# A decoder layer in split fp32: order at the end of the up projection, order of operand sums and accumulating transfers in the down pass

## The chip, the cores and the metric

The kernel runs on one core of a Trainium2 chip. The metric is the device time of one execution in microseconds (us). A core has five engines that run side by side, each through a queue of its own in order: TensorE (PE in the profile) multiplies matrices, VectorE (DVE) and ScalarE (ACT) work on rows, GpSimd (POOL) does elementwise work and issues transfers, and SyncE (SP) issues most transfers. An instruction that waits on a semaphore holds all that stands behind it on its engine. In the profile a group of instructions is named by line, engine, operation and `out<-in`.

## The reference

One step of a hybrid decoder layer: 1024 prompt rows and 64 sample rows, width 1024, feed-forward width 2816, all in fp32. Attention comes first; what matters here is the feed-forward part and the layer's end:

```python
def conv_ffn(n, prev, lw):
    a = n @ lw['ffn_w_gate']
    c = n @ lw['ffn_w_up']
    T = a.shape[1]
    full = jnp.concatenate([prev.astype(a.dtype), a], axis=1)
    w = lw['ffn_conv_w']
    conv = lw['ffn_conv_b'] + sum(w[j] * full[:, j:j + T] for j in range(CONV_W))
    y = (jax.nn.silu(conv) * c) @ lw['ffn_w_down']
    return y, full[:, full.shape[1] - (CONV_W - 1):]
...
    y, conv_new = conv_ffn(rmsnorm(h, lw['g_ffn']), conv_prev, lw)
    h = h + y
    h = h + (p.astype(h.dtype) @ lw['ple_w_proj']) * jax.nn.sigmoid(rmsnorm(h, lw['g_ple']) @ lw['ple_w_gate'])
```

The first product is called the gate branch (it passes the convolution and the silu), the second the up branch. The prompt and the sample rows go through the same layer.

## The kernel before

**Arithmetic.** PE multiplies in a reduced form of fp32, so each fp32 operand is split in two: ACT casts it to a rounded high part, and DVE (now and then POOL) subtracts that from the source to leave the residue, the low part (`split`, L114; the DVE line is L116). `mm3` (L137) then makes one product of three matmuls: high with high (L138), high with low (L139), low with high (L140).

**Up projection.** `ff_chunk(f)` (L1753) handles 128 of the 2816 columns at a time, 22 chunks. The prompt rows go by a Strassen-like scheme of products `m1` to `m7` of 384 columns each, into PSUM tiles `ps_gu`; the rows that the scheme leaves over (256 of the prompt and 64 of the sample, 320 columns) go through `rest`, once for the gate branch and once, as `pu`, for the up branch. `conv` and silu give `cv`; it is multiplied by the up branch and written to DRAM as `ds[f]`. The 64 sample columns are split into `ssm`, and a chunk later PE multiplies them by the split weights `wdh`, `wdl` into `ps_ds` (`sample_weights`, `sample_rows`, L1751). After the last chunk its own sample rows follow at the very end of the up projection: PE's last work there is `m3`, `m7`, `m4`, then the 24 matmuls of `pu`, then four `ps_ds` matmuls, which need `ssm`.

**Down pass.** y is computed by a Strassen-like scheme too: seven products, in the order of `SEVEN`: 1, 5, 6, 3, 7, 2, 4. Each runs over `NK` = 11 steps `k`, and a step is 12 matmuls of 512 columns into four PSUM tiles `ps_dn` (four row tiles, three matmuls each). I write p7 for product 7. A step has four parts:

- `load(p, k)`: SP issues two transfers of 256 KB (rows of `ds`, rows of `ffn_w_down`; three in p5). In p1 they go into one of eleven lasting tiles `st2`, for the other products into a ring of five tiles `raw2` (both read `st` and `raw` in the profile).
- `operands(p, k)`: in p5, p6, p3, p7 and p4 DVE first makes a sum or difference of the new tile and `st2` (L1942, L1943, L1948, L1952 among others), and then `split` makes the operand `o`: a cast of 128x1024 on ACT, a residue of 128x1024 on DVE. `o` has four places.
- `summed`: the matmuls.
- `folded` and `folded_on`: after a product DVE (ACT for some) adds the PSUM tiles into `h`.

`residue(i, j, t)` (L1969) is a GpSimd-issued transfer that adds 256 KB from DRAM (`dhp`, the residual stream) to a tile of `h` that was folded. There are 16 of them, and a tuple of four entries (product, first step, i, j) says where they stand in the program: four each, on every second step, in p6, p3, p7 and p2. `fold_sample` brings the sample rows' `ps_ds` into `hs` (a COPY `fd` on ACT, two additions `hs` on DVE); it stands at p1, step 1.

**Order.** The kernel is built with a scheduler that simulates a time line: it keeps the dependencies, gives each engine's instructions an order of its own and sets the waits. `tc.issue_after(x)` adds a dependency for order alone. Loads are issued four steps ahead in the program and operands two steps ahead, but on each engine the scheduler decides what really stands ahead of what.

```python
        if i + 4 < len(steps):
            load(*steps[i + 4])
        if i + 2 < len(steps):
            operands(*steps[i + 2])
```

Of the kernel before, what the change touches and what calls it, by code (L numbers as in the profile page):

```python
# [44 lines left out]
def step_kernel(ctx: ExitStack, tc: tile.TileContext, A):  # L45
# [66 lines left out]
        return r  # L112

    def split(hi, lo, src, lo_eng=None):  # L114
        act.copy(hi, src)  # L115
        (lo_eng or dve).tensor_tensor(lo, src, hi.bitcast(F32), ALU.subtract)  # L116

    def norm_rows(wk, x, rows, gb, out=None):
        junk = wk.tile([P, D], BF16, tag="sqd", name="junk", bufs=1)
# [246 lines left out]
    def sample_weights():  # L366

        hl = [cp.tile([P, 8, P], F32R, tag="craw", name="wqe", bufs=3).rearrange("p a c -> p (a c)")[:, 0:768]
              .rearrange("p (k c) -> p k c", k=2) for _ in range(3)]
        l1 = [cp.tile([P, 512], F32R, tag="csq", name="wql", bufs=2)[:, 0:384] for _ in range(2)]  # L370
        wq = []
        for f in range(2):
            hi = [hl[2 * f][:, k] for k in range(2)]
            lo = [l1[k] if f else hl[1][:, k] for k in range(2)]
            for k in range(2):
                raw = wp.tile([P, 384], F32, tag="stage", name="stage", bufs=3)
                sp.dma_start(raw, A["mla_w_qup"][0][k * P:(k + 1) * P, f * 384:(f + 1) * 384])
                split(hi[k], lo[k], raw, pool)
            wq.append((hi, lo))
        return wq  # L380
# [1372 lines left out]
    def ff_chunk(f):  # L1753
        tp = z["tp"]
        w = wgu.pop(f)
        a = tp.tile([P, 2 + T + 80], F32, tag=f"a{f % 2}", name="a", bufs=1)
        a_s = a[:, 2 + T:].rearrange("p (b t) -> p b t", t=10)
        cv = tp.tile([P, NTOK], F32, tag=f"cv{f % 2}", name="cv", bufs=1)
        cvs = cv[:, T:].rearrange("p (b t) -> p b t", t=8)
        w3 = [convT[:, j * NF + f:j * NF + f + 1] for j in range(4)]  # L1760

        def conv(n0, n1):
            dve.tensor_scalar(cv[:, n0:n1], a[:, n0:n1], w3[0], w3[3], ALU.mult, ALU.add)
            for j in (1, 2):
                dve.scalar_tensor_tensor(cv[:, n0:n1], a[:, n0 + j:n1 + j], w3[j], cv[:, n0:n1], ALU.mult, ALU.add)
# [34 lines left out]
        dve.tensor_tensor(a[:, 2 + NP:2 + 2 * NP], m3, q, ALU.add)  # L1800
        m7 = product("s3", "t3")
        dve.tensor_tensor(v, m7, v, ALU.add)
        pool.tensor_tensor(m5c, m5c, v, ALU.add)
        if late:
            sample_rows(late.pop(0), 1)
        sample_weights(f, 1)
        m4 = product("u1", "t4")
        dve.tensor_tensor(v, m4, v, ALU.add)
# [4 lines left out]
        pool.tensor_tensor(cv[:, 0:NP], cv[:, 0:NP], v, ALU.mult)  # L1813
        conv(NP, T)
        dve.tensor_scalar(cvs, a_s[:, :, 0:8], w3[0], w3[3], ALU.mult, ALU.add)
        for j in (1, 2):
            dve.scalar_tensor_tensor(cvs, a_s[:, :, j:j + 8], w3[j], cvs, ALU.mult, ALU.add)
        pool.tensor_copy(cout[:, 0:2, f], a[:, T:T + 2])
        pool.tensor_copy(cout[:, 2:18, f].rearrange("p (b j) -> p b j", j=2), a_s[:, :, 8:10])
        act.activation(cv[:, NP:], cv[:, NP:], AF.Silu)  # L1820
        pool.tensor_tensor(cv[:, NP:2 * NP], cv[:, NP:2 * NP], m5c, ALU.mult)
        dve.tensor_tensor(cv[:, 2 * NP:], cv[:, 2 * NP:], pu[:, :NR], ALU.mult)
        (pool if f == NF - 1 else sp).dma_start(ds[f], cv[:, 0:T])
        ss_ = tp.tile([P, P], F32R, tag="ssm", name="ssm", bufs=2)
        if f == NF - 1:
            dve.tensor_copy(ss_[:, 0:R], cv[:, T:])
        else:
            act.copy(ss_[:, 0:R], cv[:, T:])
        dve.tensor_tensor(ss_[:, R:2 * R], cv[:, T:], ss_[:, 0:R].bitcast(F32), ALU.subtract)
        chunks[f] = ss_  # L1830
        late.append(f)

# [81 lines left out]
    def cols_of(e, j, k):  # L1914
# [5 lines left out]
    st, src, opd, acc = {}, {}, {}, {}  # L1920

    def place_of(k):
        return f"st{(k + 3) % NK}"
# [14 lines left out]
    def operands(p, k):  # L1938

        (r, x), s2 = src.pop((p, k)), st[k]  # L1940
        if p == 5:
            dve.tensor_tensor(s2[:, 1], r[:, 1], s2[:, 1], ALU.subtract)  # L1942
            dve.tensor_tensor(s2[:, 0], r[:, 0], x, ALU.add)  # L1943
        elif p == 6:
            dve.tensor_tensor(s2[:, 1], r[:, 1], s2[:, 1], ALU.subtract)
            dve.tensor_tensor(s2[:, 0], s2[:, 0], r[:, 0], ALU.subtract)
        elif p == 7:
            dve.tensor_tensor(r, r, s2, ALU.subtract)  # L1948
        elif p == 4:
            dve.tensor_tensor(r[:, 1], r[:, 1], s2[:, 1], ALU.subtract)  # L1950
        elif p == 3:
            dve.tensor_tensor(r[:, 0], r[:, 0], s2[:, 0], ALU.subtract)  # L1952
        o = oroom()
        split(o[:, 0], o[:, 1], s2 if p in (5, 6) else r)
        opd[p, k] = o

    def banks(n):

# [1 line left out]
        return [b([P, 512], "ps_dn") for b in kinds]  # L1960

    def summed(p, k, t):
        o, tt = opd[p, k], slice(t * P, t * P + P)
# [93 lines left out]
    for i, (p, k) in enumerate(steps):  # L2057
# [169 lines left out]
```

## Time and profile before

| what | value |
| --- | --- |
| time, three runs | 2222.29, 2226.15, 2227.77 us, median 2226.15 |
| the profiled execution | 2226.47 us, its span 2224.8 us |
| mean granted TensorE clock | 0.983 |
| PE busy | 2136.6 us, 96% of the span |
| DVE, ACT, POOL busy | 1664.0, 1368.8, 1228.6 us |
| up projection ends, down pass ends, on PE | about 1872.7 us, about 2086 us |

The profile is one execution with a time stamp for each instruction. The span is the time from its first to its last record; the other 1.7 us of the execution lie around it. The view of windows gives, for each engine, its busy time and its number of instructions in a stretch, then the granted clock, the mean busy share of the 16 DMA engines and the GB/s that they moved. The time line lists instructions in order of start with the idle time ahead of them in brackets, and what ended it. SPq, DVEq and so on are an engine's sequencer.

### The profile page before, as it was taken

Reading aid. Unit: us, or ns where it says so; the run is one execution under the profiler, and the core shown is the slowest. Engines: PE = TensorE matmul, PEld = TensorE weight load, DVE = VectorE, ACT = ScalarE, POOL = GpSimd, SP = SyncE. Lnnn points to the kernel's source line nnn. Section 1 sums busy time; section 2 is a strip of 40 time slices with the busy share of each in tenths; the row PEclk is TensorE's granted clock in tenths of the full one; section 3 lists DMA queues with packets and bytes.
Section 4 is the critical chain, followed back from the end, with each engine's and each line's share of the span. In section 5 each row is a group of like instructions: output and inputs, shape, how many; then the busy total and the mean of one; then the engine's idle time right before and its main releaser. Section 6 shows DMA issues by size and latency. Waiting matters only on the chain.

```text
span 2224.8 us, 38405 instructions
## 1 busy us (share of the span) xinstructions
PE 2136.6 (96%) x13460; PEld 1932.1 (87%) x13460; DVE 1664.0 (75%) x2551; ACT 1368.8 (62%) x3726; POOL 1228.6 (55%) x1330
## 2 busy tenths in 40 slices
PE   7999989999999999999999987999999999999999
PEld 6889978878888888887888976999999998887899
DVE  4675666467788888886878778888888886976642
ACT  6576766777778888887767766333333333533631
POOL 5675668576777767777445547656565662010100
PEclk9899999999999999999999988999999999999999
DMA  5343235412342222221522212332232225958321
GB/s 181 109 142 108 77 120 157 138 54 76 96 119 72 65 60 60 61 58 52 169 69 72 70 67 91 100 104 87 96 94 93 93 91 178 298 163 233 109 70 41
DMA packets 204419, 233.07 MB, mean 105 GB/s; under 512 B 42423, under 2 KB 146340, under 8 KB 204228
## 3 DMA queue, kind: packets, MB, share of 16 engines
q1 hardware_dynamic: 188259, 179.49, 25.9%
q0 software_dynamic: 14736, 46.67, 7.4%
q10 hardware_dynamic: 1232, 4.46, 0.5%
q8 instruction: 108, 1.77, 0.3%
q14 instruction: 84, 0.68, 0.1%
HBM read 188.00 MB, written 42.52 MB: 104 GB/s over the span
## 4 chain that ended last, share of the span: by engine, by line
PE 77%; DVE 8%; ACT 5%; POOL 3%; DMA 3%; issue 2%; SPq 0%; ACTq 0%; DVEq 0%; POOLq 0%
PE ps_gu L139 7%; PE ps_gu L140 7%; PE ps_gu L138 7%; PE ks L138 5%; PE ks L140 4%; PE ks L139 4%; PE ps_dn L139 2%; PE ps_dn L140 2%; PE ps_dn L138 2%; PE cpv L644 2%; PE ctp L521 2%; PE ps_pj L138 2%; PE ps_lt L277 2%; PE ps_pj L139 2%; PE ps_pj L140 2%
## 5 line engine op out<-in xcount | busy, mean ns | idle before, releaser
L559 ACT ACTIVATE csq<-ks 128x256 f32<-128x256 f32 x1040 | 392.5, 400 | 87.1 <-PE ks L140 76.2
L564 DVE TENSOR_REDUCE css<-csq 128x16 f32<-128x1024 f32 (+1 forms) x264 | 315.7, 1196 | 64.3 <-ACT csq L559 61.4
L115 ACT CAST wh<-st 128x512 fp32r<-128x512 f32 x176 | 108.4, 619 | 187.5 <-PE ps_gu L139 167.8
L138 PE MATMUL ks<-mv1h,cTh 128*128 128x320 f32 (+1 forms) x520 | 170.0, 329 | 8.3 <-ACT sn L561 3.6
L138 PE MATMUL ks<-mv0h,cTh 128*128 128x320 f32 (+1 forms) x520 | 171.1, 331 | 7.0 <-ACT sn L561 3.0
L603 POOL TENSOR_TENSOR chl<-craw,chl 128x1024 fp32r<-128x1024 f32 x64 | 141.3, 2207 | 57.4 <-ACT chl L602 55.6
L139 PE MATMUL ks<-mv1l,cTh 128*128 128x320 f32 (+1 forms) x520 | 153.6, 297 | 0.0
L139 PE MATMUL ks<-mv0l,cTh 128*128 128x320 f32 (+1 forms) x520 | 152.4, 295 | 0.0
L140 PE MATMUL ks<-mv0h,cTl 128*128 128x320 f32 (+1 forms) x520 | 148.0, 297 | 0.9 <-DVE cTl L116 0.8
L140 PE MATMUL ks<-mv1h,cTl 128*128 128x320 f32 (+1 forms) x520 | 148.3, 299 | 0.0
L629 POOL TENSOR_TENSOR phl<-sn,phl 128x512 fp32r<-128x512 f32 (+1 forms) x64 | 85.0, 1328 | 105.5 <-ACT phl L628 104.9
L116 DVE TENSOR_TENSOR wl<-st,wh 128x512 fp32r<-128x512 f32 x132 | 119.0, 903 | 27.1 <-ACT wh L115 27.1
L116 POOL TENSOR_TENSOR wl<-st,wh 128x512 fp32r<-128x512 f32 x44 | 69.5, 1582 | 103.7 <-ACT wh L115 103.7
L139 PE MATMUL ps_dn<-o 128*128 128x512 f32 x308 | 120.6, 392 | 1.8 <-DVE o L116 1.8
L140 PE MATMUL ps_dn<-o 128*128 128x512 f32 x308 | 120.2, 390 | 0.0
L116 DVE TENSOR_TENSOR cTl<-ctp,cTh 128x512 fp32r<-128x512 f32 (+1 forms) x136 | 90.1, 662 | 38.9 <-ACT cTh L115 37.9
L138 PEld LDWEIGHTS ks<-mv1h,cTh 128*128 128x128 f32 x520 | 99.3, 191 | 20.8 <-ACT sn L561 7.7
L138 PEld LDWEIGHTS ks<-mv0h,cTh 128*128 128x128 f32 x520 | 98.2, 189 | 21.1 <-ACT sn L561 7.6
L561 ACT COPY sn<-ks 128x64 f32<-128x64 f32 x520 | 116.5, 224 | 0.0
L1316 POOL TENSOR_TENSOR pl<-p,ph 128x512 fp32r<-128x512 f32 (+1 forms) x96 | 97.5, 1020 | 30.2 <-DVE ph L1315 20.8
L138 PE MATMUL ps_dn<-o 128*128 128x512 f32 x308 | 111.1, 390 | 1.2 <-ACT o L115 1.2
L140 PE MATMUL ps_gu<-xrh,wl 128*128 128x320 f32 x352 | 108.7, 309 | 0.0
(672 smaller groups left out, 7873.3 us busy)
## 6 DMA issues: line engine op xcount, KB each, us to landing
raw<-ds SPq DMA_DIRECT2D x77, 256.0 KB
raw<-ffn_w_down SPq DMA_DIRECT2D x66, 256.0 KB
stage<-w_in SPq DMA_DIRECT2D x48, 256.0 KB
st<-ffn_w_gate SPq DMA_DIRECT2D x44, 256.0 KB
st<-ffn_w_up SPq DMA_DIRECT2D x44, 256.0 KB
wr<-ffn_w_down SPq DMA_DIRECT2D x44, 256.0 KB
ds<-cv SPq DMA_DIRECT2D x21, 512.0 KB
oraw<-doT SPq DMA_DIRECT2D x16, 256.0 KB
```

The costliest lines, as they stand in the source:

```text
L115: act.copy(hi, src)
L116: (lo_eng or dve).tensor_tensor(lo, src, hi.bitcast(F32), ALU.subtract)
L138: pe.matmul(ps, ah, bh, start=first, stop=False)
L139: pe.matmul(ps, ah, bl, start=False, stop=False)
L140: return pe.matmul(ps, al, bh, start=False, stop=last)
L277: pe.matmul(ps, x, w, start=first, stop=last)
L559: act.activation(sq[:, f * 256:f * 256 + 256], ks[:, 0:256], AF.Square)
L561: act.copy(o.sn[:, g0 + i, :], ks[:, 256:320])
L564: dve.tensor_reduce(o.ss[:, g0 + i + 1 - n:g0 + i + 1, :].rearrange("p i h -> p (i h)"), sq2[:, :n].rearrange("p i (h n) -> p (i h) n", n= ...
L603: pool.tensor_tensor(ch[:, c0:c1, 128:256], src, ch[:, c0:c1, 0:128].bitcast(F32), ALU.subtract)
L629: pool.tensor_tensor(phl[:, :nt, 64:128], sb, phl[:, :nt, 0:64].bitcast(F32), ALU.subtract)
L1316: pool.tensor_tensor(pl[:, c0:], p[:, c0:], ph[:, c0:].bitcast(F32), ALU.subtract)
```

## The change

At the end of the up projection, in the last chunk alone, the second half of the previous chunk's sample rows and the last sample weights come ahead of `m3`, and `pu` comes third from the end, ahead of `m7` and `m4`; convolution, silu, the up product of the remaining rows and the split into `ssm` follow `pu` at once. At the start of the down pass three places of `st2` are reserved in another order, so that each tile falls on the place that is released first; `fold_sample` is placed behind the cast of the last operand issued by then. In the down pass each operand sum is ordered behind the residue of the operand two before it; every accumulating transfer waits for the cast of the newest operand; and the four accumulating transfers of p7 move to p2, which now has eight, one in every step from 1 to 8.

```diff
     def split(hi, lo, src, lo_eng=None):
-        act.copy(hi, src)
-        (lo_eng or dve).tensor_tensor(lo, src, hi.bitcast(F32), ALU.subtract)
+        cast = act.copy(hi, src)
+        res = (lo_eng or dve).tensor_tensor(lo, src, hi.bitcast(F32), ALU.subtract)
+        return cast.ins, res.ins
...
+        if f == NF - 1:
+            sample_rows(late.pop(0), 1)
+            sample_weights(f, 1)
         m3 = product("s4", "22")
         dve.tensor_tensor(a[:, 2 + NP:2 + 2 * NP], m3, q, ALU.add)
...
+        if last:
+            pu = up_rest()
+            convolved()
+            gated_rest(pu)
         m7 = product("s3", "t3")
...
         m4 = product("u1", "t4")
...
-        pu = rest(w, ("u0", "u1"), both)
+        if not last:
+            pu = up_rest()
         pool.tensor_tensor(cv[:, 0:NP], cv[:, 0:NP], v, ALU.mult)
...
     def operands(p, k):
 
         (r, x), s2 = src.pop((p, k)), st[k]
-        if p == 5:
...
+        with tc.issue_after(opd[-2][1]) if len(opd) > 1 else nullcontext():
+            if p == 5:
...
         o = oroom()
-        split(o[:, 0], o[:, 1], s2 if p in (5, 6) else r)
-        opd[p, k] = o
+        opd.append(split(o[:, 0], o[:, 1], s2 if p in (5, 6) else r))
+        ops[p, k] = o
...
-        pool.dma_start(h[:, 4 * i + t, cs], dhp[rows, cs], accum_op=ALU.add)
+        d = pool.dma_start(h[:, 4 * i + t, cs], dhp[rows, cs], accum_op=ALU.add)
+        tc.add_manual_dep(d.ins, opd[-1][0].name, mybir.DependencyInfo(mybir.DependencyClass.Sync, mybir.DependencyReason.DATA),
+                          reason="one transfer at a time")
...
     z["xs"].tile([P, 2, 512], F32, tag="r", name="raw2", bufs=5)
+    for k in (10, 9, 8):
+        z["xs"].tile([P, 2, 512], F32, tag=place_of(k), name="st2", bufs=1)
...
-        for p0, k0, i_, j_ in ((6, 2, 1, 1), (3, 3, 0, 0), (7, 3, 0, 1), (2, 3, 1, 0)):
+        for p0, k0, i_, j_ in ((6, 2, 1, 1), (3, 3, 0, 0), (2, 1, 0, 1), (2, 2, 1, 0)):
             if p == p0 and k >= k0 and (k - k0) % 2 == 0 and k - k0 < 8:
                 residue(i_, j_, (k - k0) // 2)
         if p == 1 and k == 1:
-            for half in range(2):
-                fold_sample(acc_s[half], half)
+            with tc.issue_after(opd[-1][0]):
+                for half in range(2):
+                    fold_sample(acc_s[half], half)
```

DVE at the end of the last chunk and the start of the down pass, before (L1798 adds m5, L1800 m3, L1802 m7, L1808 m4; L1763 and L1765 are the convolution; L1822 multiplies by `pu`; L1454 and L1455 fold the sample rows; L116 is a residue, of weights or of an operand):

```order
L1800 TENSOR_TENSOR a<-ps_gu,q 128x384
L1763 TENSOR_SCALAR cv<-a,convT 128x640
L1765 SCALAR_TENSOR_TENSOR cv<-a,convT,cv 128x640
L1802 TENSOR_TENSOR v<-ps_gu,v 128x384
L1765 SCALAR_TENSOR_TENSOR cv<-a,convT,cv 128x640
L116 TENSOR_TENSOR wdl<-wr,wdh 128x512
L1808 TENSOR_TENSOR v<-ps_gu,v 128x384
L1822 TENSOR_TENSOR cv<-cv,ps_gu 128x320
L1826 CAST ssm<-cv 128x64
L1829 TENSOR_TENSOR ssm<-cv,ssm 128x64
L1454 TENSOR_TENSOR hs<-hs,fd 64x512
L1455 TENSOR_TENSOR hs<-hs,ps_ds 64x512
```

The same place of the changed kernel (its line numbers differ: L1804 adds m3, L1821 multiplies by `pu`, L1833 adds m7, L1840 m4):

```order
L116 TENSOR_TENSOR wdl<-wr,wdh 128x512
L1804 TENSOR_TENSOR a<-ps_gu,q 128x384
L1764 TENSOR_SCALAR cv<-a,convT 128x640
L1766 SCALAR_TENSOR_TENSOR cv<-a,convT,cv 128x640 x2
L1821 TENSOR_TENSOR cv<-cv,ps_gu 128x320
L1823 CAST ssm<-cv 128x64
L1826 TENSOR_TENSOR ssm<-cv,ssm 128x64
L1833 TENSOR_TENSOR v<-ps_gu,v 128x384
L1840 TENSOR_TENSOR v<-ps_gu,v 128x384
L116 TENSOR_TENSOR o<-st_24258,o 128x1024
L116 TENSOR_TENSOR o<-st_24261,o 128x1024
```

The pair that makes `ssm` stood behind the additions of m7 and m4 and now stands ahead of both; the additions into `hs`, which stood ahead of the first operand's residue, now stand behind the residues of the first four.

DVE at the change from p3 to p7, before. The numbers are those of the buffers: 25065, 25086, 25105 and 25126 are steps 7 to 10 of p3, and 25145, 25166, 25185 are steps 0 to 2 of p7; L116 is the residue, L1948 the sum of p7:

```order
L116 TENSOR_TENSOR o_25109<-raw2_25065,o_25109 128x1024
L1948 TENSOR_TENSOR raw2_25145<-raw2_25145,st2_24255 128x1024
L116 TENSOR_TENSOR o_25130<-raw2_25086,o_25130 128x1024
L1948 TENSOR_TENSOR raw2_25166<-raw2_25166,st2_24258 128x1024
L116 TENSOR_TENSOR o_25149<-raw2_25105,o_25149 128x1024
L1948 TENSOR_TENSOR raw2_25185<-raw2_25185,st2_24261 128x1024
```

The same place of the changed kernel (25108 and 25129 are steps 9 and 10 of p3, 25148, 25169 and 25188 steps 0 to 2 of p7, and L1972 is the sum):

```order
L116 TENSOR_TENSOR o_25152<-raw2_25108,o_25152 128x1024
L1972 TENSOR_TENSOR raw2_25148<-raw2_25148,st2_24258 128x1024
L116 TENSOR_TENSOR o_25173<-raw2_25129,o_25173 128x1024
L1972 TENSOR_TENSOR raw2_25169<-raw2_25169,st2_24261 128x1024
L116 TENSOR_TENSOR o_25192<-raw2_25148,o_25192 128x1024
L1972 TENSOR_TENSOR raw2_25188<-raw2_25188,st2_24264 128x1024
```

Before, the sum of a step stood ahead of the residue of the operand three steps earlier; now it stands ahead of the residue of the operand one step earlier. On GpSimd's queue the order is the same in both kernels.

More of the change, by code (lines that the diff above doesn't have):

```diff
@@ L1798, in ff_chunk, with up_rest, convolved, gated_rest @@
         dve.tensor_tensor(q, m5, v, ALU.add)
+        if f == NF - 1:
+            sample_rows(late.pop(0), 1)
+            sample_weights(f, 1)
         m3 = product("s4", "22")
         dve.tensor_tensor(a[:, 2 + NP:2 + 2 * NP], m3, q, ALU.add)
+        ss_ = tp.tile([P, P], F32R, tag="ssm", name="ssm", bufs=2)
+        last = f == NF - 1
+        def up_rest():
+            return rest(w, ("u0", "u1"), both)
+        def convolved():
+            conv(NP, T)
+            dve.tensor_scalar(cvs, a_s[:, :, 0:8], w3[0], w3[3], ALU.mult, ALU.add)
+            for j in (1, 2):
+                dve.scalar_tensor_tensor(cvs, a_s[:, :, j:j + 8], w3[j], cvs, ALU.mult, ALU.add)
+            pool.tensor_copy(cout[:, 0:2, f], a[:, T:T + 2])
+            pool.tensor_copy(cout[:, 2:18, f].rearrange("p (b j) -> p b j", j=2), a_s[:, :, 8:10])
+            act.activation(cv[:, NP:], cv[:, NP:], AF.Silu)
+        def gated_rest(pu):
+            dve.tensor_tensor(cv[:, 2 * NP:], cv[:, 2 * NP:], pu[:, :NR], ALU.mult)
+            if last:
+                dve.tensor_copy(ss_[:, 0:R], cv[:, T:])
+            else:
+                act.copy(ss_[:, 0:R], cv[:, T:])
+            dve.tensor_tensor(ss_[:, R:2 * R], cv[:, T:], ss_[:, 0:R].bitcast(F32), ALU.subtract)
+        if last:
+            pu = up_rest()
+            convolved()
+            gated_rest(pu)
         m7 = product("s3", "t3")
@@ L1805, in ff_chunk @@
             sample_rows(late.pop(0), 1)
-        sample_weights(f, 1)
+        if not last:
+            sample_weights(f, 1)
         m4 = product("u1", "t4")
@@ L1811, in ff_chunk @@
             gate_rest()
-        pu = rest(w, ("u0", "u1"), both)
+        if not last:
+            pu = up_rest()
         pool.tensor_tensor(cv[:, 0:NP], cv[:, 0:NP], v, ALU.mult)
[L1814 to L1820, printed above, removed]
-        pool.tensor_tensor(cv[:, NP:2 * NP], cv[:, NP:2 * NP], m5c, ALU.mult)
[L1822 to L1829, printed above, removed]
+        if not last:
+            convolved()
+        pool.tensor_tensor(cv[:, NP:2 * NP], cv[:, NP:2 * NP], m5c, ALU.mult)
+        if not last:
+            gated_rest(pu)
+        (pool if last else sp).dma_start(ds[f], cv[:, 0:T])
         chunks[f] = ss_
@@ L1940, in operands @@
         (r, x), s2 = src.pop((p, k)), st[k]
-        if p == 5:
[L1942 to L1952, printed above, removed]
+        with tc.issue_after(opd[-2][1]) if len(opd) > 1 else nullcontext():
+            if p == 5:
+                dve.tensor_tensor(s2[:, 1], r[:, 1], s2[:, 1], ALU.subtract)
+                dve.tensor_tensor(s2[:, 0], r[:, 0], x, ALU.add)
+            elif p == 6:
+                dve.tensor_tensor(s2[:, 1], r[:, 1], s2[:, 1], ALU.subtract)
+                dve.tensor_tensor(s2[:, 0], s2[:, 0], r[:, 0], ALU.subtract)
+            elif p == 7:
+                dve.tensor_tensor(r, r, s2, ALU.subtract)
+            elif p == 4:
+                dve.tensor_tensor(r[:, 1], r[:, 1], s2[:, 1], ALU.subtract)
+            elif p == 3:
+                dve.tensor_tensor(r[:, 0], r[:, 0], s2[:, 0], ALU.subtract)
         o = oroom()
-        split(o[:, 0], o[:, 1], s2 if p in (5, 6) else r)
-        opd[p, k] = o
+        opd.append(split(o[:, 0], o[:, 1], s2 if p in (5, 6) else r))
+        ops[p, k] = o
     def banks(n):
```

4 lines of the change are left out of this document (2 added, 2 removed).

## The prediction

> **What bounds the kernel now.** I read the page's head first, then the view of windows over the part that the change touches, then the time line of TensorE there, and last DVE, ACT, SP and the transfers in the places where TensorE stops.
>
> ```profile
> span 2224.8 us, 38405 instructions
> PE 2136.6 (96%) x13460; PEld 1932.1 (87%) x13460; DVE 1664.0 (75%) x2551; ACT 1368.8 (62%) x3726; POOL 1228.6 (55%) x1330
> 1870.00:1876.00 6.00, 3.12 (x14) 1.85 (x12) 3.56 (x7) 3.27 (x6) 0.67 (x1) 1.00 0.99 356
> 1876.00:2006.00 130.00, 130.00 (x577) 107.14 (x578) 108.88 (x133) 61.93 (x75) 11.50 (x14) 1.00 0.78 244
> 2006.00:2018.00 12.00, 10.72 (x45) 7.96 (x45) 10.00 (x9) 4.20 (x4) 0.00 (x0) 1.00 0.76 223
> 2018.00:2097.00 79.00, 79.00 (x386) 66.21 (x385) 51.36 (x62) 38.37 (x64) 13.11 (x20) 1.00 0.55 164
> 2097.00:2220.00 123.00, 123.00 (x1048) 122.80 (x1047) 46.45 (x84) 38.47 (x84) 0.00 (x0) 1.00 0.22 70
> ```
>
> TensorE is the bound: from 1876 us on it is busy for the whole of three of the four windows, at a granted clock of 1.00. The change takes no matmul away. So all that it can give back is the time in which TensorE stops, and that lies in two short windows. Pace without a stop: 130.00 us for 577 matmuls of 512 columns, 0.225 us each, so a step of twelve takes 2.70 us; in proportion to the columns, one of 384 takes 0.17 and one of 320 takes 0.14.
>
> ```profile
> 1870.36 0.31 PE L140 MATMUL ps_gu<-xrh,wl 128*128 128x320 f32 x1
> 1871.90 0.47 PE L1751 MATMUL ps_ds<-wdh,ssm 128*128 128x512 f32 x1 [1.23 <-DVE ssm L1829]
> 1872.66 0.40 PE L1751 MATMUL ps_ds<-wdl,ssm 128*128 128x512 f32 x1
> 1874.21 1.19 PE L138 MATMUL ps_dn<-o 128*128 128x512 f32 x4 [1.15 <-ACT o L115]
> 1875.90 0.50 PE L139 MATMUL ps_dn<-o 128*128 128x512 f32 x1 [0.50 <-DVE o L116]
> ...
> 2006.96 0.61 PE L138 MATMUL ps_dn<-o 128*128 128x512 f32 x2
> 2008.50 0.50 PE L139 MATMUL ps_dn<-o 128*128 128x512 f32 x1 [0.93 <-DVE o L116]
> ...
> 2016.58 0.39 PE L138 MATMUL ps_dn<-o 128*128 128x512 f32 x1
> 2017.32 0.50 PE L139 MATMUL ps_dn<-o 128*128 128x512 f32 x1 [0.35 <-DVE o L116]
> ```
>
> The brackets understate a stop, since a matmul's modelled end is late; I take start to start, less the pace. (a) 1.54 - 0.14 = 1.40 waiting for `ssm`; (b) 1.55 - 0.23 = 1.32 waiting for the first operand's cast; (c) 1.69 - 4 x 0.225 = 0.79 for its residue; (d) 1.54 - 0.45 = 1.09 and (e) 0.74 - 0.23 = 0.51 for residues in p7. Together 5.11 us, 0.23% of the time: the cap on any gain.
>
> **Part 1, the end of the up projection.** Matmuls change places, none is added, so `m4` ends where `pu` ended, at 1870.36 + 0.14 = 1870.50.
>
> ```profile
> 1860.29 0.33 PE L138 MATMUL ps_gu<-x22h,wh 128*128 128x384 f32 x1
> 1862.57 0.56 DVE L1800 TENSOR_TENSOR a<-ps_gu,q 128x384 f32<-128x384 f32 x1 [0.96 <-PE ps_gu L140]
> 1866.03 0.79 ACT L1820 ACTIVATE cv<-cv 128x704 f32<-128x704 f32 x1 [0.54 <-DVE cv L1765]
> 1867.34 0.54 DVE L1808 TENSOR_TENSOR v<-ps_gu,v 128x384 f32<-128x384 f32 x1
> 1870.78 0.49 DVE L1822 TENSOR_TENSOR cv<-cv,ps_gu 128x320 f32<-128x320 f32 x1 [2.89 <-PE ps_gu L140]
> 1871.53 0.23 DVE L1829 TENSOR_TENSOR ssm<-cv,ssm 128x64 fp32r<-128x64 f32 x1
> ```
>
> Two `ps_ds` matmuls (0.45) now stand ahead of `m3`, so its addition starts at 1862.57 + 0.45 = 1863.02. From there to the silu it was 3.46, with the addition of m7 in between; that is kept as an upper bound: silu at 1866.48, done at 1867.27. `pu` ends at 1860.29 + 0.45 + 12 x 0.17 + 24 x 0.14 = 1866.1, earlier. The product by `pu`, the cast and the subtraction took 0.98 from 1870.78 to 1871.76, so `ssm` stands at about 1868.3, 2.2 us before it is wanted at 1870.50. Stop (a) goes: +1.40. Even a chain 2 us longer would be covered by `m7` and `m4`.
>
> ```profile
> 1864.47 0.33 SPq L1930 DMA_DIRECT2D st<-ds  x1
> 1872.63 0.58 ACT L1453 COPY fd<-ps_ds 64x512 f32<-64x512 f32 x1 [5.81 <-PE ps_ds L1751]
> 1873.12 1.04 ACT L115 CAST o<-st 128x1024 fp32r<-128x1024 f32 x1
> 1874.64 1.21 DVE L116 TENSOR_TENSOR o<-st,o 128x1024 fp32r<-128x1024 f32 x1
> 1985.68 2.90 DMA raw<-ffn_w_down
> 2004.38 7.00 DMA raw<-ffn_w_down
> ```
>
> The first load of the down pass was issued at 1864.47, when a matmul of `m7` had released its place; its place is now one that the last matmul of `m5` releases, just before 1860.29. I take 1860.5. With landings between 2.9 and 7.0 us it is there by 1867.5; the cast (1.04) follows the silu of 1867.27 and no longer stands behind the COPY `fd`, which waited for the `ps_ds` matmuls. It is done by about 1868.5, for use at 1870.50 + 4 x 0.225 = 1871.40. Stop (b) goes: +1.32. The COPYs come after four casts; their PSUM tiles are wanted again at the earliest in p5, eleven steps or 29.7 us later.
>
> The residue stands directly behind the addition of `m4` on DVE: `m4` is added from 1870.78, when `pu` was read before, until 1871.32 (0.54 as m4's row above); the residue alone takes 1.21, until 1872.53. The four matmuls high by high last until 1871.40 + 4 x 0.225 = 1872.30. Left: 0.23. But the same addition also releases GpSimd's last multiply (L1813), which is then beside it. What that costs is seen in the up projection:
>
> ```profile
> 1858.82 0.69 DVE L116 TENSOR_TENSOR wdl<-wr,wdh 128x512 fp32r<-128x512 f32 x1 [0.32 <-ACT wdh L115]
> 1865.35 1.52 POOL L1803 TENSOR_TENSOR m<-m,v 128x384 f32<-128x384 f32 x1 [8.74 <-DVE v L1802]
> 1865.91 1.50 DVE L116 TENSOR_TENSOR wdl<-wr,wdh 128x512 fp32r<-128x512 f32 x1
> L1813 POOL TENSOR_TENSOR cv<-cv,v 128x384 f32<-128x384 f32 x21 | 29.8, 1421 | 0.0
> ```
>
> A residue of 512 elements took 0.69 alone and 1.50 beside one GpSimd multiply: 0.81 more. So 0 to 0.81 is added here; I take 0.81, since the multiply is of the same size and starts in the same moment: a stop of 1.04, where (c) was 0.79. The start gives 1.40 + 1.32 + 0.79 - 1.04 = +2.47.
>
> The Trainium skill, page "SBUF — State Buffer", section "Who interferes with whom", calls the port pair that VectorE and GpSimd share "an exclusive lock". By that the residue would wait for the whole multiply; the 1.50 row is not a full wait for a multiply that began 0.56 earlier, which would end at 1866.87 and give 1.65, but it is near. As a mechanism of this kernel it is a rival below.
>
> **Part 2, the stops in p7.**
>
> ```profile
> 2006.09 1.23 DVE L1948 TENSOR_TENSOR raw<-raw,st 128x1024 f32<-128x1024 f32 x1 [2.12 <-DMA raw<-ffn_w_down]
> 2007.23 2.35 DVE L116 TENSOR_TENSOR o<-raw,o 128x1024 fp32r<-128x1024 f32 x2
> 2011.50 1.23 DVE L1948 TENSOR_TENSOR raw<-raw,st 128x1024 f32<-128x1024 f32 x1 [1.92 <-DMA raw<-ffn_w_down]
> ```
>
> A sum waits 2.12 us for its load, and behind it on DVE wait two residues that TensorE wants at once. The order rows say why: the sum of a step stands ahead of the residue of three steps earlier. Its buffer, one of a ring of five, is released by the residue of five steps earlier; so a load has two steps less that residue and the sum, 5.40 - 1.21 - 1.23 = 2.96 us, and the transfer of 7.00 quoted above doesn't fit. Now the sum stands ahead of the residue of one step earlier: two steps more, 2.96 + 5.40 = 8.36 us, which holds 7.00. I count (d) and (e) as gone: +1.60. If the load were as late again, the sum would still wait, but the residue next in line would be wanted a step later.
>
> **Part 3, the accumulating transfers.** They leave p7 and come in every step of p2. In p2's window of 16 us from 2029 to 2045, the queues' rows are:
>
> ```profile
> q1 hardware_dynamic: 1651, 3.01, 53.0%
> q0 software_dynamic: 576, 1.05, 45.3%
> ```
>
> 1.05 MB are four accumulating transfers: 0.453 x 16 / 4 = 1.81 us of all engines each. 3.01 MB are 11.5 loads: 0.74 each. A step of p2 with two loads and one such transfer thus asks 3.29 us of 2.70; over eight steps the transfers fall 4.7 us behind. Low bound: an accumulating transfer costs as a load does, 2.22 a step, nothing is late. What covers it: from the residue that frees a buffer to the cast that needs it again are five steps less a residue and a cast, 13.5 - 1.21 - 1.04 = 11.25 us; less the 7.00 landing there are 4.25 to spare. So 0.45 us at most come through; p2 makes no sums (its operands are cast as they land), so no residue is held by one. I take 0. The wait of the transfers on a cast holds GpSimd's queue, on which in p2 nothing else stands; the tiles of `h` that they fill are read a product later, in p4.
>
> The sum: 2.47 + 1.60 = 4.1 us. From the profiled execution's 2226.47 that is 2222.4; the median of the runs, 2226.15, is 0.3 below it, and gives **2222.1**.
>
> **Rivals.**
> 1. *GpSimd doesn't disturb the residue*, because DVE starts first or the multiply has ended. The stop is 0.23 instead of 1.04: 4.9 gained, 2221.2 from the median. For it: operand residues of 1.21 stand in the quoted rows with POOL busy 0.67 of 6 us. Against: all is released by one addition.
> 2. *GpSimd holds DVE off altogether*: the residue starts 1.42 late, at 1872.74, ends at 1873.95, stop 1.65: 3.5 gained, 2222.7. The section named above would have it so.
> 3. *The stops in p7 move instead of going*: whichever sum meets the late load holds one residue still. Then only the start counts, 2.5, 2223.6. For it: the 7.00 row; against: the transfers that crowded the loads have left p7.
> 4. *Slower: p2 runs out of transfers.* If one accumulating transfer costs more than (2.70 - 1.48) + (4.25 + 4.1) / 8 = 2.26 us of the engines, the backlog eats the reserve and the whole gain. At 3.2 us it would be 8 x 1.98 = 15.8 late, 11.6 after the reserve, and the kernel 7.5 slower: 2233.6. Against it stands the 1.81; for it, that TensorE ran through p2 with half as many.
>
> That the change does not do what it says is ruled out by the order rows.
>
> **Chances.** Forecast 0.45, rival 1 0.20, rival 2 0.12, rival 3 0.13, rival 4 0.10. The three runs spread over 5.5 us, so a median may sit 2 to 3 us off; the range runs from 2218.6 (2221.2 less that) to 2226.8, which leaves out most of rival 4 and little else. A difference under 0.3%, 6.7 us, is about what a measurement of this kernel can't tell from no change; the border on the fast side is 2219.5, 1.7 below rival 1 and 2.6 below the forecast, within the scatter of a median: 0.27 for faster, nearly all from these two; 0.66 for no difference; 0.07 for slower by that much, the far half of rival 4 and scatter on top of its near half.
>
> **What would show it.** In the trace of the changed kernel: no stop ahead of the first `ps_ds` matmul of the last chunk, `ssm` 2 us early; the first cast `o` before 1870; the first residue on DVE at 1.2 (rival 1), about 2.0 (forecast), or late by 1.4 (rival 2); TensorE without a gap in p7, the sums' wait for loads gone or harmless; in p2 the share of the transfer engines near 1.0 and, for rival 4, casts that wait for `raw`. The prediction is wrong if TensorE stops anywhere from p5 to p4 for over 1 us, or if its pace leaves 0.225.

## The result, and the profile after

| what | before | changed kernel |
| --- | --- | --- |
| median of ten runs | 2226.95 us (2222.29 to 2229.06) | 2220.51 us (2218.33 to 2223.21) |
| ratio, 95% interval | 1 | 0.9975 [0.9965, 0.9985] |
| span of the profiled execution | 2224.8 us | 2219.6 us |

The ratio is that of the means: the changed kernel is 0.25% faster (0.15% to 0.35%), some 5.6 us. The medians lie 6.4 apart, and the forecast, from median to median, was 4.1. The page's head of the changed kernel, and the windows of the same stage as before (busy time by engine, granted clock, share of the transfer engines, GB/s):

```profile
span 2219.6 us, 38384 instructions
```

```profile
1870.00:1876.00 6.00, 5.93 (x27) 4.71 (x27) 4.86 (x5) 2.85 (x4) 4.36 (x4) 1.00 1.05 391
1876.00:2006.00 130.00, 130.00 (x579) 107.20 (x578) 114.23 (x139) 60.77 (x76) 8.26 (x10) 1.00 0.78 242
2006.00:2018.00 12.00, 12.00 (x55) 9.94 (x54) 7.76 (x7) 4.32 (x5) 0.00 (x0) 1.00 0.60 200
2018.00:2097.00 79.00, 79.00 (x405) 66.92 (x404) 49.11 (x61) 41.13 (x70) 16.69 (x24) 1.00 0.54 157
```

TensorE's busy time went from 3.12 to 5.93 us in the first window and from 10.72 to 12.00 in the third. What is left of the five stops stands in the time line of TensorE at the start of the down pass:

```profile
1870.70 0.34 PE L141 MATMUL ps_gu<-xt4h,wl 128*128 128x384 f32 x1
1870.87 0.39 PE L1752 MATMUL ps_ds<-wdh,ssm 128*128 128x512 f32 x1
...
1871.79 1.09 PE L139 MATMUL ps_dn<-o 128*128 128x512 f32 x4
1872.95 0.50 PE L140 MATMUL ps_dn<-o 128*128 128x512 f32 x1
```

No stop ahead of `ps_ds`, none ahead of `ps_dn`; four matmuls of 0.227 after 1871.79 would end at 1872.70, so 0.25 us remain ahead of the low matmuls, where 0.79 had been.

To compare kernels I use a stretch that leaves out the scatter of the 1860 us ahead of it: from the start of `m5`'s last matmul to the start of the last `ps_dn` matmul.

```profile
1860.11 0.33 PE L140 MATMUL ps_gu<-xt1h,wl 128*128 128x384 f32 x1
...
2091.37 0.40 PE L140 MATMUL ps_dn<-o 128*128 128x512 f32 x1
```

```profile
1860.45 0.34 PE L141 MATMUL ps_gu<-xt1h,wl 128*128 128x384 f32 x1
...
2086.31 0.40 PE L141 MATMUL ps_dn<-o 128*128 128x512 f32 x1
```

The first pair is the kernel before, 231.26 us; the second is the changed kernel, 225.86 us: 5.40 less. That splits into 2.76 up to the first `ps_dn` matmul, 0.51 in p1 and 2.13 in p7 (first matmul of a product to first matmul of the next: p7 took 32.05 and now takes 29.92, as p5, p6, p3 and p2 do in both kernels).

### The profile page after: what moved, and what is told of

Read it like the earlier page. It is cut to its first block, busy times and chain, and to the rows that moved or that the text cites. A ratio compares the mean times of both kernels' runs of the same rounds, so it can differ in the third digit from the quotient of the medians.

```text
span 2219.6 us, 38384 instructions
## 1 busy us (share of the span) xinstructions
PE 2134.6 (96%) x13460; PEld 1934.7 (87%) x13460; DVE 1666.6 (75%) x2551; ACT 1369.1 (62%) x3726; POOL 1227.5 (55%) x1330
## 4 chain that ended last, share of the span: by engine, by line
PE 80%; DVE 7%; ACT 5%; DMA 4%; POOL 2%; issue 2%; SPq 0%; DVEq 0%; POOLq 0%; ACTq 0%
PE ps_gu L140 7%; PE ps_gu L141 7%; PE ps_gu L139 7%; PE ks L139 5%; PE ks L141 5%; PE ks L140 4%; PE ps_dn L141 3%; PE ps_dn L140 3%; PE ps_dn L139 3%; PE cpv L645 2%; PE ctp L522 2%; PE ps_lt L278 2%; PE ps_pj L139 2%; PE ps_pj L140 1%; PE ps_pj L141 1%
## 5 line engine op out<-in xcount | busy, mean ns | idle before, releaser
L116 DVE TENSOR_TENSOR wl<-st,wh 128x512 fp32r<-128x512 f32 x132 | 119.0, 903 | 28.5 <-ACT wh L115 28.5
L116 POOL TENSOR_TENSOR wl<-st,wh 128x512 fp32r<-128x512 f32 x44 | 69.4, 1580 | 103.5 <-ACT wh L115 98.2
L116 DVE TENSOR_TENSOR cTl<-ctp,cTh 128x512 fp32r<-128x512 f32 (+1 forms) x136 | 90.1, 663 | 39.4 <-ACT cTh L115 38.4
L139 PE MATMUL ps_gu<-xrh,wh 128*128 128x320 f32 x352 | 108.6, 309 | 1.1 <-ACT xrh L115 1.1
```

What stands on the lines that cost most here:

```text
L116: res = (lo_eng or dve).tensor_tensor(lo, src, hi.bitcast(F32), ALU.subtract)
L139: pe.matmul(ps, ah, bh, start=first, stop=False)
```

## The experiments

The stretch, and p7, of every run, worked out in that way, each figure from one profile:

| run | stretch, us | p7, us |
| --- | --- | --- |
| kernel before (and two more profiles of it) | 231.26 (231.79, 235.41) | 32.05 (32.57, 34.55) |
| changed kernel | 225.86 | 29.92 |
| end of up projection undone | 226.91 | 29.92 |
| sums free | 230.69 | 31.90 |
| transfers undone | 225.84 | 29.92 |
| first residue ahead of m4's addition | 225.48 | 29.92 |
| places free | 230.37 | 29.92 |
| fold_sample free | 231.46 | 29.92 |
| transfers of p2 doubled | 227.33 | 29.92 |
| sums free and transfers undone | 230.02 | 34.07 |
| a long GpSimd multiply ahead of the residue | 226.59 | 29.92 |
| kernel before with ordered sums alone | 230.76 | 29.92 |

Among the versions the timed runs tell little apart: the ratios to the kernel before lie between 0.9973 and 0.9987 with intervals of about 0.0013 to each side; a run without a ratio below was executed once, for its profile. The start of `m5`'s last matmul alone lies between 1854.7 and 1864.1 us in these profiles, over instructions that all versions share.

**The end of the up projection undone.** `pu` comes last again, and the sample rows and weights of the last chunk go back behind `m7`; the down pass is kept as changed.

```diff
-        if f == NF - 1:
-            sample_rows(late.pop(0), 1)
-            sample_weights(f, 1)
...
-        if last:
-            pu = up_rest()
-            convolved()
-            gated_rest(pu)
         m7 = product("s3", "t3")
...
-        if not last:
-            sample_weights(f, 1)
+        sample_weights(f, 1)
         m4 = product("u1", "t4")
         dve.tensor_tensor(v, m4, v, ALU.add)
...
+        pu = rest(w, ("u0", "u1"), both)
```

> The changed kernel with the end of the up projection as before (pu last), all else kept. Theory (the parts are independent, each stop belongs to one edit): only the wait for ssm comes back, 1.40 us of stop ahead of the first ps_ds matmul; the casts of o, now ahead of the fd copies, are done while PE runs the ps_ds matmuls, so no stop of 1.3 ahead of ps_dn; p7 without a stop. Time: about 1.2 to 1.6 us over the changed kernel. Rival (the order of pu is what makes room for the first loads and casts): the stop ahead of ps_dn comes back too, 2.7 us or more in all.

The theory's stop came back and no other. TensorE's time line:

```profile
1874.33 0.31 PE L141 MATMUL ps_gu<-xrh,wl 128*128 128x320 f32 x1
1875.87 0.47 PE L1752 MATMUL ps_ds<-wdh,ssm 128*128 128x512 f32 x1 [1.23 <-DVE ssm L1830]
...
1876.88 1.09 PE L139 MATMUL ps_dn<-o 128*128 128x512 f32 x4
```

1.54 from start to start, as in the kernel before; then TensorE runs on. The stretch grew by 1.05 only, since the wait for `ssm` also gives the first residue time: the 0.25 of the changed kernel and the slow matmul behind it are gone. Timed: 0.9973 [0.9960, 0.9986].

**Places free.** The three reserved `st2` places are left out.

```diff
-    for k in (10, 9, 8):
-        z["xs"].tile([P, 2, 512], F32, tag=place_of(k), name="st2", bufs=1)
```

> The changed kernel without the three reserved places: the first load of the down pass again waits for a matmul near the end of m7, about 8 us later than in the changed kernel. Theory (early loads are what removes the stop ahead of ps_dn): first cast late by the landing of 3 to 7 us, a stop of 1.5 to 5 us ahead of the first ps_dn matmul. Rival (casts ahead of the fd copies are enough): under 0.5 us.

ACT and SP in that run, with TensorE behind them:

```profile
1869.74 0.34 SPq L1953 DMA_DIRECT2D st<-ds  x1
...
1874.81 1.04 ACT L115 CAST o<-st 128x1024 fp32r<-128x1024 f32 x1 [6.11 <-DMA st<-ffn_w_down]
```

```profile
1875.91 1.84 PE L139 MATMUL ps_dn<-o 128*128 128x512 f32 x4 [3.04 <-ACT o L115]
1877.55 0.63 PE L140 MATMUL ps_dn<-o 128*128 128x512 f32 x1
1877.97 0.63 PE L141 MATMUL ps_dn<-o 128*128 128x512 f32 x1
```

The load is issued at 1869.74 instead of 1860.82 and the first cast waits for it: a stop of 3.20 from start to start, less the pace. The edit of the places is needed because of the edit of `pu`: `m7`, whose matmuls release the old place, now comes after `pu`. The matmuls behind the stop start 0.43 apart instead of 0.23; that is taken up below.

**fold_sample free.** The order edge behind the last cast is left out.

```diff
-            with tc.issue_after(opd[-1][0]):
+            with nullcontext():
                 for half in range(2):
```

> The changed kernel with fold_sample free to come first: both fd copies stand ahead of the first cast on ACT and the hs additions ahead of the first residue on DVE; loads still early. Theory (casts first matters by itself): two copies of 0.58 after the last ps_ds matmul, then the cast of 1.04, so a stop of about 2.3 to 2.7 ahead of the first ps_dn matmul and 0.3 to 0.7 for its residue. Rival: the early loads alone are enough, stop under 0.5.

ACT in that run, the columns as before:

```profile
1871.87 0.58 ACT L1454 COPY fd<-ps_ds 64x512 f32<-64x512 f32 x1 [3.87 <-PE ps_ds L1752]
...
1873.75 0.58 ACT L1454 COPY fd<-ps_ds 64x512 f32<-64x512 f32 x1 [1.29 <-DVE hs L1455]
...
1874.23 1.04 ACT L115 CAST o<-st 128x1024 fp32r<-128x1024 f32 x1
```

The second copy waits for the first addition on DVE, since both use one `fd` tile, and the cast stands behind both. Apart from one small transpose TensorE has nothing to do until 1875.33; the stretch is 5.6 us longer, more than the theory's 2.6 to 3.4, and part of it is again matmuls at half pace. Early loads and casts first are both needed.

**Sums free**, the transfers as in the changed kernel:

```diff
-        with tc.issue_after(opd[-2][1]) if len(opd) > 1 else nullcontext():
+        with nullcontext():
```

> The changed kernel without the order edge on the operand sums; the accumulating transfers stay moved and spread. In p7 a sum stands again three residues early on DVE. Theory A (the order of sums is what removed the stops of p7): a late load is again felt by a residue, p7 takes 1 to 2 us more than its 29.92 and PE waits for DVE residues there. Theory B (the transfers, moved out of p7, are what removed them): loads land within 3 us in p7 since no accumulating transfer is beside them, p7 stays at 29.92.

**Transfers undone**, the sums as in the changed kernel: `residue` without its wait, and the tuple of the kernel before.

```diff
-        d = pool.dma_start(h[:, 4 * i + t, cs], dhp[rows, cs], accum_op=ALU.add)
-        tc.add_manual_dep(d.ins, opd[-1][0].name, mybir.DependencyInfo(mybir.DependencyClass.Sync, mybir.DependencyReason.DATA),
-                          reason="one transfer at a time")
+        pool.dma_start(h[:, 4 * i + t, cs], dhp[rows, cs], accum_op=ALU.add)
...
-        for p0, k0, i_, j_ in ((6, 2, 1, 1), (3, 3, 0, 0), (2, 1, 0, 1), (2, 2, 1, 0)):
+        for p0, k0, i_, j_ in ((6, 2, 1, 1), (3, 3, 0, 0), (7, 3, 0, 1), (2, 3, 1, 0)):
```

> The changed kernel with the accumulating transfers as before: four of them in p7, no wait on a cast, so that they come in bursts; the sums keep their new order. Theory A (order of sums): p7 stays at 29.92, though the loads beside the burst again take about 7 us; some sums wait for loads and no residue that PE wants is behind them. Theory B (transfers): p7 takes 1 to 2 us more. If neither this run nor the one with free sums has stops in p7, either edit alone was enough.

Theory A holds in both. With the sums free, DVE in the first step of p7 shows the pattern of before although no accumulating transfer stands in p7; TensorE's row follows the two of DVE:

```profile
1988.67 1.23 DVE L1972 TENSOR_TENSOR raw<-raw,st 128x1024 f32<-128x1024 f32 x1 [2.56 <-DMA raw<-ffn_w_down]
1989.81 1.22 DVE L116 TENSOR_TENSOR o<-raw,o 128x1024 fp32r<-128x1024 f32 x1
```

```profile
1991.08 0.50 PE L140 MATMUL ps_dn<-o 128*128 128x512 f32 x1 [0.62 <-DVE o L116]
```

The sum of step 4 waits 2.56 us, and the residue of step 1 behind it reaches TensorE late. Two such stops stood in p7, which took 1.98 more; a small one stood in p2, and the longest in p4, ahead of transposes, while the sums of p4 waited for their loads. The stretch was 4.8 us longer. With the transfers undone and the sums ordered, the bursts are back and one sum in p7 waits, as the two views show, time line of GpSimd and list of waits:

```profile
1989.72 0.86 POOL L1993 DMA_DIRECT2D h<-dhp  x1 [24.58 <-DVE h L2010]
1992.59 2.64 POOL L1993 DMA_DIRECT2D h<-dhp  x3 [2.01 <-DVE h L2010]
```

```profile
DVE raw L1972 <- DMA raw<-ffn_w_down: 1.6, 1, 1.6
```

No residue that TensorE wants is behind it; p7 took 29.92. The moving and spreading of the transfers brought nothing that can be seen here.

**Both undone.** The sums are free, `residue` has no wait, and the tuple is that of the kernel before.

```diff
-        with tc.issue_after(opd[-2][1]) if len(opd) > 1 else nullcontext():
+        with nullcontext():
...
-        d = pool.dma_start(h[:, 4 * i + t, cs], dhp[rows, cs], accum_op=ALU.add)
...
+        pool.dma_start(h[:, 4 * i + t, cs], dhp[rows, cs], accum_op=ALU.add)
...
-        for p0, k0, i_, j_ in ((6, 2, 1, 1), (3, 3, 0, 0), (2, 1, 0, 1), (2, 2, 1, 0)):
+        for p0, k0, i_, j_ in ((6, 2, 1, 1), (3, 3, 0, 0), (7, 3, 0, 1), (2, 3, 1, 0)):
```

> The changed kernel with both edits of the down pass undone (sums free, transfers as before), the start kept. Theory (order of sums decides, and the earlier transfers of p7 set the size): p7 takes about 2.1 us over 29.92 as in the kernel before, the other products 29.92 or nearly; p4 without the stops that the run with free sums and moved transfers had. Rival: stops elsewhere, as in that run, 3 us or more.

The stops were in p7 alone, so the theory's place was right, but p7 took 4.15 us more and not 2.1: one stop was longer (2.37 beyond the pace), and what followed it was slow. TensorE's time line:

```profile
2003.79 0.61 PE L139 MATMUL ps_dn<-o 128*128 128x512 f32 x2
2006.61 0.50 PE L140 MATMUL ps_dn<-o 128*128 128x512 f32 x1 [2.21 <-DVE o L116]
...
2008.51 0.63 PE L139 MATMUL ps_dn<-o 128*128 128x512 f32 x1
2008.94 0.63 PE L140 MATMUL ps_dn<-o 128*128 128x512 f32 x1
```

**Ordered sums alone**, in the kernel before:

```diff
+        with tc.issue_after(opd[-2][1]) if len(opd) > 1 else nullcontext():
+            if p == 5:
...
+        opd.append(split(o[:, 0], o[:, 1], s2 if p in (5, 6) else r))
...
```

> The kernel before with the order edge on the operand sums alone. Theory (that edge alone removes the stops of p7): p7 takes 29.92 us instead of 32.05, the three stops at the start of the down pass stay as before (1.4, 1.3 and 0.7), 2.1 us less than the kernel before from the end of m5 to the end of the down pass, hardly visible in the timed runs. Rival (it needs the moved or spread transfers as well): p7 stays above 31.

p7 took 29.92: that edge alone removes its stops. The three stops at the start were there with 1.39, 1.33 and 0.66 (the third is 0.66 in the kernel before too, from the last start ahead of it; the 0.79 of the prediction counts from the first of the four matmuls), but the stretch was only 0.5 us shorter than in the first profile of the kernel before, since here the clock fell behind them. Timed: 0.9987 [0.9972, 1.0001].

**The kernel before, twice more.** Nothing is edited.

> The kernel before once more, unchanged, for a second profile of its three stops at the start of the down pass. In its first profile the granted clock stayed at 1.00 behind them; in the run with the order edge on the sums alone, whose start is the same, it fell to 0.57 for one window of 4 us. Theory (the clock falls by chance of a window that these stops fall into, so the kernel before pays it in some executions): a clock between 0.5 and 0.9 in some window from the first stop to 10 us behind it in one or both of two more profiles, with 1.5 to 1.8 us more in p1. Rival (it was that run's own): 1.00 in both.

> As the run before this one, a third profile of the kernel before: the theory has a clock under 0.9 behind the stops in one or both of the two, the rival 1.00 in both.

In one of the two the clock fell, behind the start and again behind p7's stop; the windows of that profile, with the granted clock ahead of the last two columns:

```profile
1870.00:1874.00 4.00, 2.50 (x8) 1.73 (x9) 3.75 (x6) 3.10 (x6) 0.00 (x0) 0.89 1.05 382
1874.00:1878.00 4.00, 4.00 (x13) 3.16 (x13) 3.35 (x4) 3.56 (x5) 0.95 (x2) 0.68 1.05 403
2005.00:2009.00 4.00, 1.32 (x6) 0.82 (x5) 2.69 (x3) 1.05 (x1) 0.00 (x0) 1.00 1.10 236
2009.00:2013.00 4.00, 4.00 (x12) 3.11 (x12) 2.87 (x3) 0.35 (x1) 0.00 (x0) 0.59 0.89 285
```

Its stretch was 235.41, against 231.79 in the other and 231.26 in the first. p7's stops differ as well, since they hang on when a load lands: 2.84 in one piece here, 1.48 and 0.56 there, 1.09 and 0.51 in the first.

**A long GpSimd multiply ahead of the residue.** It squares a tile that is not used any more.

```diff
+        summed5 = pool.tensor_tensor(m5c, m5c, v, ALU.add)
+        if last:
+            with tc.issue_after(summed5.ins):
+                long_one = pool.tensor_tensor(a[:, 0:T], a[:, 0:T], a[:, 0:T], ALU.mult)
...
+        with tc.issue_after(long_one.ins) if last else nullcontext():
+            pool.tensor_tensor(cv[:, 0:NP], cv[:, 0:NP], v, ALU.mult)
...
+        with tc.issue_after(long_one.ins) if last else nullcontext():
+            pool.tensor_tensor(cv[:, NP:2 * NP], cv[:, NP:2 * NP], m5c, ALU.mult)
```

> The changed kernel with one more GpSimd multiply (128x1024, of a tile that is no longer needed) between its last addition and its last two multiplies, so that it runs from about 1870.8 when the first operand's residue is issued on DVE at 1871.6. At 1.02 us for 384 elements it takes about 2.7. Theory 1 (an instruction with two operands in SBUF that starts second waits for the whole of the other engine's one): the residue ends about 1.1 to 1.2 after the long multiply, near 1874.6 instead of 1872.9, and TensorE stops for 1.8 to 2.1 us ahead of the low matmuls instead of 0.24. Theory 2 (both slow down while they overlap, by 0.81 for each overlap): the residue takes about 2.0, a stop of 0.9 to 1.2. Theory 3 (no effect on the residue): 0.24.

DVE and GpSimd in that run:

```profile
1866.85 1.90 POOL L1837 TENSOR_TENSOR a<-a 128x1024 f32<-128x1024 f32 x1
...
1867.80 3.98 DVE L116 TENSOR_TENSOR o<-st,o 128x1024 fp32r<-128x1024 f32 x2
1868.70 2.00 POOL L1854 TENSOR_TENSOR cv<-cv,m 128x384 f32<-128x384 f32 x1
...
1869.88 0.50 PE L140 MATMUL ps_dn<-o 128*128 128x512 f32 x1 [0.82 <-DVE o L116]
1870.66 1.99 POOL L1850 TENSOR_TENSOR cv<-cv,v 128x384 f32<-128x384 f32 x1
```

The long multiply took 1.90 instead of the 2.7 expected, so the stop (1869.88 - 1867.97 - 4 x 0.227 = 1.00) rules out theory 3 but doesn't tell the other two apart: by theory 1, with 1.90, the residue ends 1.1 to 1.2 after 1868.75, by theory 2 it lasts 2.0, and both come to about 1869.85. The second GpSimd multiply, issued at 1868.70, ends at 1870.70, and the third, issued at 1870.66, at 1872.65, each about 2.0, though a multiply of that size took 1.01 alone (in the kernel before, with DVE idle beside it). That fits both theories too:

```profile
1868.26 1.01 POOL L1813 TENSOR_TENSOR cv<-cv,v 128x384 f32<-128x384 f32 x1
```

What tells them apart is whether the one that starts first keeps its pace. In the changed kernel's own profile DVE starts first; the first residue keeps its pace, nearly, while the multiply waits:

```profile
1871.62 1.27 DVE L116 TENSOR_TENSOR o<-st,o 128x1024 fp32r<-128x1024 f32 x1
```

```profile
1871.78 1.99 POOL L1846 TENSOR_TENSOR cv<-cv,v 128x384 f32<-128x384 f32 x1
```

1.27 against 1.21 alone for the one that started first; 1.99 against 1.01 for the one 0.16 later: 1871.62 + 1.27 = 1872.89, and 0.88 later the multiply ends. If each slowed the other the first would not keep its pace. So theory 1: the two take turns, a whole instruction each. The Trainium skill, page "SBUF — State Buffer", section "Who interferes with whom", says just that, with the sentence "Issue order, not op shape, decides who blocks"; these rows agree.

**The first residue ahead of m4's addition**, the version that these readings point to:

```diff
-        dve.tensor_tensor(v, m4, v, ALU.add)
+        z["m4_added"] = dve.tensor_tensor(v, m4, v, ALU.add).ins
...
     operands(*steps[0])
+    tc.add_manual_dep(z["m4_added"], opd[0][1].name, mybir.DependencyInfo(mybir.DependencyClass.NoSync, mybir.DependencyReason.DATA),
+                      reason="issue_after")
```

> The changed kernel with the first operand's residue ordered ahead of m4's addition on DVE. Theory: it runs from about 1869.6 to 1870.8, while DVE would wait for m4, and the last stop at the start of the down pass (0.24, with 0.11 more for the matmul after it) goes: 0.3 to 0.4 us less than the changed kernel between the end of m5 and the end of the down pass, not visible in the timed runs. Rival (GpSimd's work beside it stretches it or is stretched so that m4's addition and the last multiply come late and something else stops): a new stop in p1.

The residue starts at 1869.73 and takes 1.22; TensorE runs from `m4` into `ps_dn` without a stop, no new stop stands in p1, and the stretch is 225.48, 0.38 less than the changed kernel. Timed: 0.9975 [0.9962, 0.9989], not to be told from it. The run also shows the turns once more:

```profile
1869.73 1.22 DVE L116 TENSOR_TENSOR o<-st,o 128x1024 fp32r<-128x1024 f32 x1
1869.96 1.87 POOL L1834 TENSOR_TENSOR m<-m,v 128x384 f32<-128x384 f32 x1 [12.75 <-ACT o L115]
```

The residue, which started first, kept its pace; the GpSimd addition 0.23 behind it took 1.87, where it took 1.01 in the run with the long multiply, with nothing beside it.

**The transfers of p2 doubled.** The residual is added twice to half of the tiles.

```diff
-        d = pool.dma_start(h[:, 4 * i + t, cs], dhp[rows, cs], accum_op=ALU.add)
+        for _ in range(2 if (i, j) in ((0, 1), (1, 0)) else 1):
+            d = pool.dma_start(h[:, 4 * i + t, cs], dhp[rows, cs], accum_op=ALU.add)
...
```

> The changed kernel with each accumulating transfer of p2 issued twice (the residual is added twice to half of the tiles): 16 in p2. Theory (the engines of the transfers are a limit of p2 and the ring of five buffers is the reserve): a step asks 2 x 0.76 + 2 x 1.50 = 4.5 us of 2.72, 14.4 us behind after eight steps; with a reserve of 4.3 to 8.4, TensorE stops for 6 to 10 us in p2 and early p4, with casts that wait for raw, and the kernel is 6 to 10 us slower than the changed one. Rival (accumulating transfers are throttled by their own queue and do not hold the loads up): under 2 us.

The theory fell, and the rival's under 2 us held. p2 took 29.92, no cast waited for its load there, and the kernel was 1.5 us slower in the stretch. Queues from 2022 to 2064, and the wait that mattered, from the list of waits:

```profile
q0 software_dynamic: 2090, 3.82, 51.3%
q1 hardware_dynamic: 3889, 7.08, 49.1%
```

```profile
ACT junk L1465 <- DMA h<-dhp: 5.5, 1, 5.5
```

The engines of the transfers were full (51.3% and 49.1%), but the loads came in time; the accumulating transfers fell behind, and what felt it was the first reader of `h` in p4; p4 took 1.45 more, with one stop ahead of its transposes. One limit of this run: the two transfers of a tile write the same place, so the second waits on GpSimd until the first has landed (seven such waits from 2022 to 2075, 26.1 us together), while in the changed kernel the transfers of p2 wait for casts alone. What sixteen transfers without that wait would do to the loads is not shown.

## Why the prediction was right

The direction, the range and the places were right: all five stops were waits for the operands named, four went, one shrank. The range alone says little, since it ran from 7.5 us less to 0.7 more; the traces carry the account. The sum was low, 4.1 of 5.6, and its misses, at stop (c), in p7 and in the cap, all go the same way.

- **Stop (a), 1.40.** `ssm` stood at 1868.62 (1868.3 forecast), 2.25 us ahead of its use. The run with `pu` last gives 1.39 back.
- **Stop (b), 1.32.** Gone, and by the two causes named, early loads and casts first: without either one it is back, and longer.
- **Stop (c).** Forecast 1.04 left, 0.25 measured. This is the term that was mis-sized: the 0.81 for GpSimd beside the residue. The row it came from was a residue that had started second; here it started first, by 0.16 us, and GpSimd paid. Rival 1 had this stop with 0.23, because DVE starts first, and for the start of the down pass that is what happened: with 0.23 in place of 1.04 the prediction's terms give 3.28, and the stretch shows 2.76 + 0.51 = 3.27.
- **Stops (d) and (e), 1.60.** Gone by the order of the sums, as argued; the rival in which they move did not come. That the transfers had left p7, which I held against that rival, was no part of the cause: with them back p7 stayed at 29.92. Of the two reasons given, more time for the load and no wanted residue behind the sum, the second is enough: with the transfers back one sum still waited 1.6 us for a load of 7.9, so the 8.36 us counted for a load did not hold there, and TensorE did not stop. Worth 2.13 in p7, not 1.60: p7 had a third, small stop that I did not count, ahead of the low matmuls of step 6 (2013.62 to 2013.91), and the first matmul behind each of the three costs 0.11 more, as told below.
- **Accumulating transfers, 0.** Right, but as far as the doubled transfers show, not because the loads have 4.25 us to spare. One costs 1.50 us of the engines when spread (0.354 x 34 / 8 by the row below, for the window from 2018 to 2052 of the changed kernel) and not 1.81, so a step asks 3.0 us of 2.72, still too much; but what was late in the doubled run is the transfers themselves and not the loads. Rival 4 had the wrong victim: with twice the transfers p2 did not lose a microsecond, with the limit told of that run.

```profile
q0 software_dynamic: 1152, 2.10, 35.4%
```

- **The cap of 5.11.** It was too low, for two reasons. The first matmul behind a stop of the down pass is started 0.34 before the next instead of 0.23, so a stop costs 0.11 more than its gap (for (b) that is already in the 0.79 of (c)). And it came from one execution: of four profiles with the three stops at the start (three of the kernel before, one with ordered sums alone) two show a fallen clock behind them, and a p1 of 33.72 and 33.73 us where the first profile had 32.11: 1.6 us more each. The kernel before thus loses more on average than its first profile shows, and the measured 5.6 (3.3 to 7.8) doesn't need another cause. How often the clock falls in its timed runs was not measured.

## What to carry to other kernels

Behind a load that may be late, look at what stands next on the engine that waits: in the kernel before two sums of p7 waited about 2 us each, with residues that TensorE wanted behind them, and p7 lost 2.1 us; with the sums ordered and the transfers as before one sum still waited 1.6 us, with no wanted residue behind it, and p7 lost nothing. A stop's price is read from start to start, over more than one profile, since it depends on when a load lands and on whether the clock falls. And when an instruction's stretched time is taken as a price, see first which of the two engines had started.

## What the runs showed of the hardware

TensorE's clock fell after far less idle time than I had looked for. Behind the stop of 2.4 us in p7 (both edits of the down pass undone), some 1.5 to 1.9 us after TensorE had begun again, matmuls started 0.43 us apart instead of 0.23; eight of them in a row are 3.4 us and cost 1.6 us; in two of four profiles three stops of 1.4, 1.3 and 0.7 us within 5.6 did the same. Stops of 1.5 us or less that stood alone never did, and neither did one in p4 of the run with sums free, 2.06 from start to start. The window of the run with free places shows it most plainly:

```profile
1876.00:1880.00 4.00, 4.00 (x11) 3.13 (x12) 2.34 (x2) 1.08 (x2) 0.00 (x0) 0.57 0.92 283
```

Eleven matmuls in 4 us, where the changed kernel has seventeen or more, at a mean clock of 0.57. The Trainium skill, page "TensorE: Matmul & The Clock Gate", section "What's actually happening", tells of a free-running window of about 3.4 us after which an idle TensorE is throttled; a window that runs free fits two falls in four at the same stops, but the stop of 2.4 in p7 and the three short ones were well under a whole window of idle time, and the measurement decides.
